# Second values and gates in the background of the attention items, queries split over 128 rows

## The chip, the cores and the metric

The kernel runs on one core of one Trainium2 chip. The metric is the device time of one launch in microseconds, the median of several runs, and less is better. The core's engines work side by side, each with its own queue of instructions: TensorE (PE; its weight loads are shown as PEld), VectorE (DVE), ScalarE (ACT), GpSimd (POOL) and SyncE (SP), which here issues most DMA transfers. Matmul results go to eight PSUM banks; everything else lies in SBUF.

## The reference, cut to what matters

A decoder of two layers over 512 tokens of width 1024. Layer 0 is a short gated convolution and a squared-ReLU MLP. Its output is normed and projected once to keys and values for three attention branches; layer 1 is the attention, followed by a second MLP and a last norm. The attention has 16 heads in 4 groups (4 heads share keys and values), head size 64.

```python
h   = rms_norm(x, kv_norm);  kv = h @ w_kv          # six parts of 256 columns: raw k, raw v, sel k, sel v, win k, win v
k_cmp, v_cmp = silu(blocks(raw + pe) @ phi_w1) @ phi_w2   # 31 blocks of 32 tokens, stride 16
q   = (rms_norm(x, g) @ w_qg[:, :1024]) * 64**-0.5
gates = sigmoid(rms_norm(x, g) @ w_qg[:, 1024:])    # three per head
o_b = softmax(q k_b^T + bias + mask) v_b            # b: compressed, selected, window
o   = gates[0]*o_c + gates[1]*o_s + gates[2]*o_w;   x += o @ w_o
```

With 512 tokens the top 16 of 8 blocks are all blocks, and the window is as long as the sequence, so the second and third branch are both full causal attention, with keys and values of their own.

## The kernel before

Each float32 operand is kept as a float16 high part and a float16 rest, and a product is made of three matmuls (hi x hi, hi x rest, rest x hi; `mm3`). Weights come in pieces of 128 x 1024 float32. `pieces` lists them in the order of use (L74 to L145); SP loads a piece to a staging buffer `wst` (three of them), ACT makes its high part `whi` (L232) and DVE its rest `wlo` (L233; four buffers each). `next_piece` hands out the next one, `ahead_fine` converts up to two pieces ahead, in steps of 512 columns up to the list's index `whole`. So the list and the order of the calls have to agree.

The attention (from L760) has a **lead-in** and an **item loop**. The lead-in (L1080) runs `keys(0)`, `keys(1)`, `queries(0)`, `values(0)`, `values(1)` and `gates()` to their ends. `keys` and `values` are of the two full branches: `values` makes 4 x 8 x 3 matmuls of 256 columns into two PSUM banks and evicts four 128 x 256 tiles to `VT` (ACT high part, DVE rest). `gates` makes 96 matmuls of 48 columns and evicts with Sigmoid on ACT into `GT`. During the lead-in, `abank` takes banks in turn from three pairs; afterwards always from the pair `a`.

The loop runs over 96 **items**. A `Full` item is one query block (128 tokens, index `qb`), one branch `br` and one, two or four heads; a `Cmp` item is one query block of the compressed branch for the eight heads of two groups. `items` (L1297) has the 22 Full items of group 0, those of group 1, then groups 2 and 3 with four Cmp items mixed into each. An item has five steps: `st0` scores (L1152, L1153), bias and minimum (DVE, L1160), Exp (ACT, L1162); `st1` transposes (L1168, PSUM bank `c`) and the high part on ACT (L1171); `st2` the rest on DVE (L1174); `st3` the product with the values (L1187 to L1189) and, at the last item of a query block, division and gates on DVE; `st4` the transposed output in `ot` once all branches of the block are in (`finish`). Iteration `i` emits st0 of item `i`, st1 of `i-2`, st2 of `i-3`, st3 of `i-4`, st4 of `i-6`.

Beside the items runs the **background** (L1303), a generator whose steps yield what they charge (0.65 for three matmuls of 512 columns; a step that names nothing is charged 0.1). Each iteration adds to `credit` and runs background until it is used up (L1334 to L1346); a "wait" sets the credit to zero. Its order: `raw(0)`, `queries(1)`, `phi(0)` in turn with `raw(1)`, `queries(2)`, `phi(1)`, `queries(3)`, and, when groups 0 and 1 are finished, `out_proj(0)`. `raw` projects raw keys or values and puts them, by transfers from `kr_hl`, into the tile `big` in the layout that `phi` (the compression MLP) reads as moving operand. `queries` projects a group's 256 query columns. `head` then makes each head's high part on ACT and the rest on DVE or POOL, 64 partitions at a time: the tile `Q` holds a head's high part in one half of the partitions and its rest in the other. Outside the lead-in the four `head` calls go to `later`, of which one runs per iteration. `queries(3)` waits with its eviction until the last Cmp item of groups 0 and 1 has been emitted, because `Q` has three buffers.

What is emitted in this order is then placed on the engines' queues by a scheduler that goes by that order as priority and by what is ready in its own plan.

Of the kernel before, what the change touches and what calls it, by code (L numbers as in the profile page):

```python
# [48 lines left out]
def body(ctx, tc, x, rel_bias, norm_mix, norm_mlp, mlp_w1, mlp_w2, a_w_in, a_conv_w, a_w_out,  # L49
# [75 lines left out]
    for part in (3, 5):  # L125
        block(w_kv, part * 256)
    cols(b_w_qg[0], 1024, 48, SW)
    block(w_kv, 0)
    block(b_w_qg[0], 256)

    for k in (0, 8):
        block(phi_k_w1, 0, SW, k, 4)
        cols(w_kv, 256, 256, SW, k // 2, 4)
        block(phi_k_w1, 0, SW, k + 4, 4)
    cols(phi_k_w2, 0, 64, SW, 0, 2)
    block(b_w_qg[0], 512)
# [623 lines left out]
    with pool("attn") as ap:  # L760
# [126 lines left out]
        def gates():  # L887
            w = next_piece()
            pg = abank()
            for t in range(4):  # L890
                for c in range(8):
                    lx = [u[:, c, t * 128:(t + 1) * 128] for u in xq]
                    o = pg[:, t * 48:(t + 1) * 48]
                    PE.matmul(o, lx[0], w[0][:, c], start=c == 0, stop=False)
                    PE.matmul(o, lx[0], w[1][:, c], start=False, stop=False)
                    PE.matmul(o, lx[1], w[0][:, c], start=False, stop=c == 7)
                yield
            for t in range(4):
                ACT.activation(GT[:, t], pg[:, t * 48:(t + 1) * 48], AF.Sigmoid, bias=zero, scale=rtok[:, 1, t:t + 1])
            DVE.tensor_scalar(GT, GT, SO / (SP * SV), None, op0=OP.mult)  # L900
            gc = GT[:, 0].rearrange("p (h b) -> p h b", b=3)[:, :, 0]
            DVE.tensor_scalar(gc, gc, any_, None, op0=OP.mult)
            yield


        def queries(g):
# [7 lines left out]
            def head(h):  # L914
# [3 lines left out]
                (POOL if g in (0, 3) else DVE).tensor_tensor(q[o, h], t[r, m], q[r, h], op=OP.subtract)  # L918
                done.add(f"q{g}.{h}")

            for m in range(2):
                DVE.tensor_tensor(t[:, m], po[m], rbq, op=OP.mult)
            for h in range(4):
                if lead_in[0]:
                    head(h)
                else:
                    later.append(lambda h=h: head(h))
# [5 lines left out]
        def raw(which):  # L933
# [3 lines left out]
            DVE.memset(kr[64:128, :, 0:4, S - 1:S], 0.0)  # L937
# [5 lines left out]
            for m in range(2):  # L943
# [6 lines left out]
                for s in range(2):  # L950
# [3 lines left out]
                    nc.sync.dma_start(kr[64:128, :, g, S - 32:S - 1], hl[r, :, 1:32])  # L954
# [72 lines left out]
        done = set()  # L1027
# [52 lines left out]
        for k in (keys(0), keys(1), queries(0), values(0), values(1), gates()):  # L1080
            drain(k)
# [50 lines left out]
        class Full:  # L1132
# [7 lines left out]
            def need(self):  # L1140
                return [f"q{self.g}.{self.heads[-1]}"]

# [64 lines left out]
        class Cmp:  # L1207
# [5 lines left out]
            def need(self):  # L1213
                return [f"q{2 * self.gp}.3", f"q{2 * self.gp + 1}.3", "cmp"]

# [82 lines left out]
        items += mixed(full(2), {4 + 3 * qb: Cmp(0, qb) for qb in range(4)})  # L1298
# [4 lines left out]
        def background():  # L1303
            yield from raw(0)
            yield from queries(1)
            yield from in_turn(phi(0), raw(1))
            yield from queries(2)
# [8 lines left out]

        lead = {1: 2, 2: 3, 3: 4, 4: 6}
        credit = 3.0
        for i in range(len(items) + 5):
            if i < len(items):  # L1320
                for k in items[i].need():
                    while k not in done:
                        if later:
                            later.pop(0)()
                        elif next(bg, "end") in ("wait", "end"):
                            raise RuntimeError(k)
# [7 lines left out]
            credit += 1.14 if i < 44 else 0.9 if i < 50 else 0.58  # L1334
# [3 lines left out]
            for part in ("stages", "background") if frees else ("background", "stages"):  # L1338
# [8 lines left out]
                for s in (1, 2, 3, 4):  # L1347
                    j = i - lead[s]
                    if 0 <= j < len(items) and (s, j) != (4, len(items) - 1):
                        getattr(items[j], f"st{s}")()  # L1350
# [177 lines left out]
```

## Time and profile before

| | |
|---|---|
| median of 3 runs | 1106.68 us (1106.1 to 1107.04) |
| profiled execution | 1106.44 us, of which span 1104.7 us |
| granted TensorE clock | 0.998 |
| lead-in of the attention | about 500 to 545 us of the span |
| item loop, first to last score matmul | 544.8 to 747.6 us |

The profile is that of one execution on the one core. Times within it count from the start of the span. [...] A row of a group gives line, engine, operation, output and inputs, shapes, count, then busy us, mean ns, and the idle time before with what ended it.

### The profile page before, as it was taken

How to read it: one execution, taken by the hardware profiler on the slowest of the kernel's cores; microseconds unless marked ns; L12 is line 12 of the kernel's file. 1: busy time of each engine (PE TensorE's matmuls, PEld its weight loads, DVE VectorE, ACT ScalarE, POOL GpSimd, SP SyncE). 2: the span in 40 equal slices, each digit the busy share in tenths (PEclk: the TensorE clock that was granted, in tenths of full speed). 3: DMA queues.
4: the chain of work that ended last, by engine and by line, in shares of the span. 5: the costliest groups of instructions: out<-in, count | busy, mean ns of one | idle time of the engine just before them, and what ended most of it. 6: DMA issues, size and time to landing. Idle time of an engine off the chain costs nothing. (4 is left out here: it accounts for less than half of the span.)

```text
span 1104.7 us, 20302 instructions
## 1 busy us (share of the span) xinstructions
PE 1087.0 (98%) x8112; PEld 704.9 (64%) x8112; DVE 897.3 (81%) x1594; ACT 584.0 (53%) x925; POOL 57.4 (5%) x74
## 2 busy tenths in 40 slices
PE   9999999999999999999999999999999999999997
PEld 4446644447884448875767676675444788445886
DVE  5897757987988767979488899996798798875786
ACT  5663245544333544447677887874655534352353
POOL 1000000000000000000100102211100000000022
PEclk9999999999999999999999999999999999999999
DMA  8353135633333333312352432011653333330222
GB/s 254 117 152 115 39 96 153 172 96 115 115 108 106 111 97 108 103 31 76 115 154 68 131 116 79 28 33 57 172 153 115 116 115 115 115 96 1 84 89 77
DMA packets 149710, 115.77 MB, mean 105 GB/s; under 512 B 8828, under 2 KB 146768, under 8 KB 149616
## 3 DMA queue, kind: packets, MB, share of 16 engines
q1 hardware_dynamic: 146720, 109.14, 33.0%
q10 hardware_dynamic: 2512, 4.70, 1.4%
q8 instruction: 64, 1.05, 0.4%
q0 software_dynamic: 384, 0.63, 0.2%
q14 instruction: 30, 0.25, 0.1%
HBM read 110.22 MB, written 2.14 MB: 102 GB/s over the span
## 5 line engine op out<-in xcount | busy, mean ns | idle before, releaser
L232 ACT ACTIVATE whi<-wst 128x1024 f16<-128x1024 f32 (+3 forms) x156 | 136.2, 887 | 120.8 <-PE b L387 37.4
L688 PEld LDWEIGHTS <-whi 128*128 128x128 f16 x1768 | 173.0, 98 | 20.4
L219 ACT ACTIVATE whi<-wst 128x1792 f16<-128x1792 f32 x70 | 118.2, 1696 | 124.6 <-DVE wst L160 55.5
L233 DVE SCALAR_TENSOR_TENSOR wlo<-wst,whi 128x1024 f16<-128x1024 f32 (+3 forms) x156 | 157.1, 1017 | 26.6 <-ACT whi L232 26.3
L388 PEld LDWEIGHTS <-wlo 128*128 128x128 f16 x976 | 95.5, 98 | 105.5 <-issue 0.7
L386 PEld LDWEIGHTS <-whi 128*128 128x128 f16 x976 | 95.7, 98 | 101.0 <-issue 0.9
L387 PEld LDWEIGHTS <-whi 128*128 128x128 f16 x976 | 95.5, 98 | 100.3 <-issue 0.3
L220 DVE SCALAR_TENSOR_TENSOR wlo<-wst,whi 128x1792 f16<-128x1792 f32 x70 | 141.0, 2018 | 15.4 <-ACT whi L219 15.4
L625 DVE TENSOR_TENSOR rl<-ml_z,rh 128x1792 f16<-128x1792 f32 x32 | 64.7, 2023 | 44.5 <-ACT rh L624 44.4
L688 PEld LDWEIGHTS <-wlo 128*128 128x128 f16 x884 | 86.5, 98 | 10.8 <-issue 0.4
L624 ACT ACTIVATE rh<-ml_z 128x1792 f16<-128x1792 f32 x32 | 54.3, 1696 | 60.2 <-DVE ml_z L166 60.2
L1162 ACT ACTIVATE at_p<-at_s,at_m 128x384 f32<-128x384 f32 (+3 forms) x128 | 70.9, 555 | 22.3 <-DVE at_m L1160 21.2
L388 PE MATMUL b<-xsh,wlo 128*128 128x512 f16 x208 | 78.8, 379 | 0.0
L387 PE MATMUL b<-xsl,whi 128*128 128x512 f16 x208 | 78.8, 379 | 0.0
L386 PE MATMUL b<-xsh,whi 128*128 128x512 f16 x208 | 78.8, 379 | 0.0
L386 PE MATMUL c<-xsh,whi 128*128 128x512 f16 x192 | 72.8, 379 | 0.0
L387 PE MATMUL c<-xsl,whi 128*128 128x512 f16 x192 | 72.8, 379 | 0.0
L388 PE MATMUL c<-xsh,wlo 128*128 128x512 f16 x192 | 72.8, 379 | 0.0
L158 DVE TENSOR_TENSOR wst<-wst 128x512 f32<-128x512 f32 x70 | 48.5, 695 | 26.5 <-DMA wst<-mlp_w_dram 25.2
L688 PE MATMUL a<-rh,whi 128*128 128x256 f16 x256 | 69.1, 273 | 0.0
L688 PE MATMUL a<-rh,wlo 128*128 128x256 f16 x256 | 69.1, 273 | 0.0
L688 PE MATMUL c<-rh,whi 128*128 128x256 f16 x252 | 68.7, 273 | 0.1
(388 smaller groups left out, 2686.8 us busy)
## 6 DMA issues: line engine op xcount, KB each, us to landing
wst<-mlp_w_dram SPq DMA_DIRECT2D x256, 256.0 KB, 3.4
wst<-a_w_in_dram SPq DMA_DIRECT2D x12, 512.0 KB, 3.8
wst<-w_kv_dram SPq DMA_DIRECT2D x12, 512.0 KB, 3.8
wst<-a_w_out_dram SPq DMA_DIRECT2D x8, 512.0 KB, 3.4
wst<-b_w_qg_dram SPq DMA_DIRECT2D x8, 512.0 KB, 3.7
wst<-b_w_o_dram SPq DMA_DIRECT2D x8, 512.0 KB, 3.4
T<-ext_d ACTq DMA_DIRECT2D x6, 528.0 KB, 3.9
wst<-a_w_in_dram SPq DMA_DIRECT2D x12, 256.0 KB, 3.0
```

The lines of the kernel that those rows point to most:

```text
L158: DVE.tensor_tensor(b[:, :, 4:7:2], b[:, :, 0:1].to_broadcast(two), b[:, :, 2:0:-1], op=OP.add)
L219: ACT.activation(hi, b[:, :, 1:], AF.Copy, scale=sc)
L220: lows[0] = DVE.scalar_tensor_tensor(lo, b[:, :, 1:], sc, hi, op0=OP.mult, op1=OP.subtract)
L232: ACT.activation(hi[:, s:e], w, AF.Copy, scale=sc)
L233: DVE.scalar_tensor_tensor(lo[:, s:e], w, sc, hi[:, s:e], op0=OP.mult, op1=OP.subtract)
L386: PE.matmul(ps, w[0], xs[0], start=start, stop=False, **k)
L387: PE.matmul(ps, w[0], xs[1], start=False, stop=False, **k)
L388: return PE.matmul(ps, w[1], xs[0], start=False, stop=stop, **k)
L624: ACT.activation(rh[0][:, p], z[:, 1:8], AF.Copy)
L625: DVE.tensor_tensor(rh[1][:, p], z[:, 1:8], rh[0][:, p], op=OP.subtract)
L688: mm = PE.matmul(acc7[i], wl if n == 1 else wh, xl if n == 2 else xh, stop=c == closes[i] and n == 2, start=c == 0 and n == 0 and not othe ...
L1162: self.weighed = ACT.activation(self.p[:, w], lg[:, w], AF.Exp, bias=mn[:, j:j + 1], scale=-1.0, accum_out=l[:, br * 4 + h:br * 4 + h + 1])
```

## The change

- The lead-in ends after `values(0)`. `values(1)` and `gates()` become the first parts of the background; a Full item's `st3` first asks for the values of its branch and, for branch 1, the gates (`need_last`, `have`). `gates` now yields a charge and converts weights ahead.
- The background's order is `values(1)`, `gates`, `queries(1)`, `raw(0)`, `phi(0)` in turn with `queries(2)`, `raw(1)`, `phi(1)`, `queries(3)`, `out_proj(0)`; the list of weight pieces follows.
- The credit per iteration is 1.25 up to item 53, 1.0 up to 63, then 0.75 (before: 1.14 up to 43, 0.9 up to 49, then 0.58).
- The four Cmp items of groups 0 and 1 stand behind Full items 9, 11, 14 and 16 of group 2 instead of 4, 7, 10 and 13.
- Queries of groups 1 to 3 are split over all 128 partitions, two heads at a time, into `kr_hl`, and four transfers put the halves into `Q`. Group 0's rests are still made per head, all on POOL.
- `raw` loses a memset and the third transfer of each group, which filled columns that no matmul reads.

```diff
     block(b_w_qg[0], 0)
-    for part in (3, 5):
-        block(w_kv, part * 256)
+    block(w_kv, 3 * 256)
+    block(w_kv, 5 * 256)
     cols(b_w_qg[0], 1024, 48, SW)
+    block(b_w_qg[0], 256)
     block(w_kv, 0)
-    block(b_w_qg[0], 256)
 
     for k in (0, 8):
         block(phi_k_w1, 0, SW, k, 4)
-        cols(w_kv, 256, 256, SW, k // 2, 4)
+        cols(b_w_qg[0], 512, 256, SW, k // 2, 4)
         block(phi_k_w1, 0, SW, k + 4, 4)
     cols(phi_k_w2, 0, 64, SW, 0, 2)
-    block(b_w_qg[0], 512)
+    block(w_kv, 256)
     block(phi_v_w1, 0, SW, 0, 16)
...
         def gates():
             w = next_piece()
+            cv = ahead_fine()
             pg = abank()
             for t in range(4):
                 for c in range(8):
+                    next(cv, None)
...
-                yield
+                yield 0.6
+            drain(cv)
...
                 ACT.activation(q[r, h], t[r, m], AF.Copy)
-                (POOL if g in (0, 3) else DVE).tensor_tensor(q[o, h], t[r, m], q[r, h], op=OP.subtract)
+                POOL.tensor_tensor(q[o, h], t[r, m], q[r, h], op=OP.subtract)
                 done.add(f"q{g}.{h}")
+
+            def two_heads(m, hl):
+                ACT.activation(hl[:, 2 * m], t[:, m], AF.Copy)
+                (POOL if g == 3 else DVE).tensor_tensor(hl[:, 2 * m + 1], t[:, m], hl[:, 2 * m], op=OP.subtract)
+
+            def put_heads(hl):
+                for s in range(2):
+                    r, o = slice(64 * s, 64 * s + 64), slice(64 - 64 * s, 128 - 64 * s)
+                    nc.sync.dma_start(q[r, s::2], hl[r, 0::2])
+                    nc.sync.dma_start(q[o, s::2], hl[r, 1::2])
+                done.update(f"q{g}.{h}" for h in range(4))
 
             for m in range(2):
                 DVE.tensor_tensor(t[:, m], po[m], rbq, op=OP.mult)
-            for h in range(4):
-                if lead_in[0]:
+            if lead_in[0]:
+                for h in range(4):
                     head(h)
-                else:
-                    later.append(lambda h=h: head(h))
+            else:
+                hl = ap.tile([128, 4, S], F16, name="kr_hl", bufs=1)
+                for m in range(2):
+                    later.append(lambda m=m: two_heads(m, hl))
+                later.append(lambda: put_heads(hl))
             yield
...
-            DVE.memset(kr[64:128, :, 0:4, S - 1:S], 0.0)
...
                     nc.sync.dma_start(kr[0:64, :, g, :], hl[r])
                     nc.sync.dma_start(kr[64:128, :, g, 0:S - 32], hl[r, :, 32:S])
-                    nc.sync.dma_start(kr[64:128, :, g, S - 32:S - 1], hl[r, :, 1:32])
...
-        for k in (keys(0), keys(1), queries(0), values(0), values(1), gates()):
+        for k in (keys(0), keys(1), queries(0), values(0)):
             drain(k)
...
+            def need_last(self):
+                return [f"v{self.br}"] + (["gates"] if self.br else [])
...
-        items += mixed(full(2), {4 + 3 * qb: Cmp(0, qb) for qb in range(4)})
+        items += mixed(full(2), {i: Cmp(0, qb) for qb, i in enumerate((9, 11, 14, 16))})
...
         def background():
+            yield from marked("v1", values(1))
+            yield from marked("gates", gates())
+            yield from queries(1)
             yield from raw(0)
-            yield from queries(1)
-            yield from in_turn(phi(0), raw(1))
-            yield from queries(2)
+            yield from in_turn(phi(0), queries(2))
+            yield from raw(1)
             yield from marked("cmp", phi(1))
...
+        def have(names):
+            for k in names:
+                while k not in done:
+                    if later:
+                        later.pop(0)()
+                    elif next(bg, "end") in ("wait", "end"):
+                        raise RuntimeError(k)
...
-            credit += 1.14 if i < 44 else 0.9 if i < 50 else 0.58
+            credit += 1.25 if i < 54 else 1.0 if i < 64 else 0.75
...
+                        if s == 3:
+                            have(items[j].need_last())
                         getattr(items[j], f"st{s}")()
```

More of the change, by code (lines that the diff above doesn't have):

```diff
@@ L1025, in phi @@
             drain(ahead())
-        done = set()
+        done = {"v0"}
         oT = {}
@@ L1214, in need, with need_last @@
                 return [f"q{2 * self.gp}.3", f"q{2 * self.gp + 1}.3", "cmp"]
+            def need_last(self):
+                return []
             def st0(self):
@@ L1320, in body @@
             if i < len(items):
[L1321 to L1326, printed above, removed]
+                have(items[i].need())
                 items[i].st0()
```

## The prediction

> **What bounds the kernel now.** The page comes first. TensorE (PE) is shown busy for 98% of the span, so a gain that isn't less matmul work has to come out of the rest.
>
> ```profile
> span 1104.7 us, 20302 instructions
> PE 1087.0 (98%) x8112; PEld 704.9 (64%) x8112; DVE 897.3 (81%) x1594; ACT 584.0 (53%) x925; POOL 57.4 (5%) x74
> ```
>
> The change touches the attention part alone, so the second view is the busy time by stretches of it. The columns are PE, weight loads, VectorE (DVE), ScalarE (ACT) and GpSimd (POOL), then the granted clock and the DMA share.
>
> ```profile
> 500.00:545.00 45.00, 45.00 (x393) 31.27 (x391) 31.55 (x62) 27.48 (x51) 5.22 (x4) 1.00 0.32 89
> 545.00:570.00 25.00, 24.27 (x194) 14.59 (x193) 18.36 (x59) 19.91 (x55) 0.00 (x0) 1.00 0.41 117
> 600.00:626.00 26.00, 24.45 (x262) 16.79 (x261) 22.02 (x74) 19.43 (x66) 0.73 (x1) 1.00 0.47 144
> ...
> 626.00:691.00 65.00, 62.64 (x793) 47.22 (x791) 63.99 (x178) 54.78 (x143) 10.36 (x14) 1.00 0.34 100
> ...
> 691.00:706.00 15.00, 12.65 (x144) 9.09 (x142) 13.39 (x41) 13.84 (x38) 6.63 (x6) 1.00 0.01 2
> ...
> 545.00:747.00 202.00, 194.47 (x2198) 139.04 (x2197) 183.91 (x542) 160.93 (x438) 26.27 (x36) 1.00 0.30 88
> ```
>
> The lead-in (500 to 545) holds PE full while DVE has 13 us free. The item loop (545 to 747) is the reverse: PE is shown idle for 202 - 194.5 = 7.5 us, and from 626 to 691 DVE works 63.99 of 65 us: there DVE, not PE, ends the work. The largest hole per us is 691 to 706, 2.35 us of 15. What PE stands still for:
>
> ```profile
> PE c L1168 <- DVE at_pl L1174: 3.5, 7, 1.1
> ...
> PEld c L1168 <- issue: 5.0, 8, 1.5
> PEld c L1168 <- DVE at_pl L1174: 2.3, 6, 0.6
> ```
>
> Mostly it is a transpose (L1168) that needs a PSUM bank which DVE (L1174) still reads. The 7.5 us are a lower bound: a matmul's shown length runs past the start of the next.
>
> ```profile
> 498.33 0.38 PE L386 MATMUL a<-xsh,whi 128*128 128x512 f16 x1
> 498.55 0.38 PE L387 MATMUL a<-xsl,whi 128*128 128x512 f16 x1
> ```
>
> A 512-column matmul is shown for 0.38 us, and the next starts after 0.22, so each stop hides up to 0.16 us. With about 40 stops (the three rows alone have 21) that is 6.4 us more. Everything that filling can win is 7.5 to 14 us, estimated from these rows.
>
> **The change, part by part.**
>
> *Second values and gates leave the lead-in.* Their PE work:
>
> ```profile
> 542.28 0.27 PE L876 MATMUL b<-whi,xsl 128*128 128x256 f16 x1
> 542.39 0.19 PE L894 MATMUL c<-whi,xqh 128*128 128x48 f16 x1
> ...
> L874 PE MATMUL b<-whi,xsh 128*128 128x256 f16 x32 | 8.7, 272 | 0.0
> ...
> L1152 PE MATMUL b<-KD,Q x128: 217/298/380, 544.8 to 747.6; 128*128 128x384 f16 x32, 128*128 128x128 f16 x32, 128*128 128x512 f16 x32, 128*128 128x256 f16 x32
> ...
> L884 DVE SCALAR_TENSOR_TENSOR VT<-b,rtok,VT x4: 477/481/482, 537.9 to 544.8; 128x256 f16<-128x256 f32 x4
> ```
>
> The values are 3 x 32 matmuls at 0.11 us from start to start, 10.5 us; the gates run from 542.39 to the first item at 544.8, 2.4 us. So the items start 12.9 us earlier, and the same 12.9 us of PE work is spread among them. This alone moves no end; it gains as much as it fills stops. What DVE takes over with it is small: 4 evictions of 0.48 us, 1.9 us, and two short gate operations.
>
> *The rate.* From L1334 and the charges that each background step yields, I count the background per iteration. Before, iterations 44 to 63 grant 6 x 0.9 + 14 x 0.58 = 13.5 us of it; after, 10 x 1.25 + 10 x 1.0 = 22.5. Counted back from iteration 65 (692.5, quoted below) at some 2.1 us each, they lie from about 648 to 691, in the stretch in which DVE ends the work. With 9 us more PE work beside the same items, its 42 us of DVE work and the 5.5 us of phi(1)'s conversions that move in (8 x 0.69) lie in some 52 us: 91% instead of 98%. Up to iteration 43 the rate rises by 0.11 only, and PE is nearly full there already. I take that of the stops from 600 to 691 (1.55 + 2.36 us shown, some 7 with what the records hide) about 2 remain: **-5.0 us**.
>
> *Queries split over 128 rows.*
>
> ```profile
> L917 ACT ACTIVATE Q<-q_t x16: 613/627/631, 523.9 to 696.8; 64x512 f16<-64x512 f32 x16
> L918 POOL TENSOR_TENSOR Q<-q_t,Q x8: 1152/1156/1496, 524.7 to 697.6; 64x512 f16<-64x512 f32 x8
> L918 DVE TENSOR_TENSOR Q<-q_t,Q x8: 684/686/687, 581.9 to 647.4; 64x512 f16<-64x512 f32 x8
> ...
> L407 ACT ACTIVATE kr_hl<-q_t x4: 612/618/623, 559.8 to 623.1; 128x512 f16<-128x512 f32 x4
> ```
>
> Half the partitions cost as much as all of them (0.627 against 0.618 us). For groups 1 and 2 DVE loses 4 x 0.686 = 2.7 us, little more than the moved evictions bring, so DVE's total stays; ACT loses 6 x 0.62 = 3.7 us. Group 3 needs two POOL operations (1.16 us) instead of four. Added are 4 transfers per group on SP's queue, between the weight loads; they are costed with the next part. Behind a transfer that waits for POOL or DVE stand those loads, which run two pieces ahead. For all of this I take 0, from -1 (DVE) to +2 (group 3, whose queries now pass two POOL operations and four transfers, some 2.3 + 2.6 + 2.3 us, within the five iterations before their first use).
>
> *The hole.* Background of group 3 waits for the last block of groups 0 and 1.
>
> ```profile
> 692.52 3.61 POOL L918 TENSOR_TENSOR Q<-q_t,Q 64x512 f16<-64x512 f32 x3 [3.48 <-issue]
> ```
>
> This is iteration 65, in the hole at 691. Before, no background is issued in iterations 64 to 68; after, the compressed items lie later (the last at 64 instead of 61) and none is issued in 65 to 71. Five iterations cost 2.35 us shown, about 3.5 with the hidden part; seven cost 4.9 by the same rate: **+1.4**, from 0 to +3.
>
> *The gates among the items.* Sigmoid and Exp need different tables on ACT.
>
> ```profile
> 544.01 0.46 ACT L883 ACTIVATE VT<-b,rtok 128x256 f16<-128x256 f32 x1
> 544.49 1.28 ACT L899 ACT_TABLE_LOAD   x1
> 545.78 1.24 ACT L899 ACTIVATE GT<-c,zero,rtok 128x48 f32<-128x48 f32 x4
> 547.04 1.28 ACT L1162 ACT_TABLE_LOAD   x1
> ```
>
> Before there are two loads; after, Exp, Sigmoid, Exp: three. The burst of 1.28 + 1.24 + 1.28 = 3.8 us now stands in front of Exps that transposes wait for. ACT works 19.9 of 25 us at that place, and a transpose comes two iterations (4.6 us) after its Exp is queued, so most is covered: +0.6, from 0 to the whole 3.8. [...]
>
> *Raw keys and values, and what stands behind them.* One memset and 8 small transfers go, of 24.
>
> ```profile
> 558.16 1.98 DVE L946 TENSOR_TENSOR q_t<-a,rb 128x512 f32<-128x512 f32 x2
> ...
> L952 SPq DMA_DIRECT2D big<-kr_hl x8: 590/606/659, 561.9 to 627.3; - x8
> L954 SPq DMA_DIRECT2D big<-kr_hl x8: 601/610/1197, 563.3 to 628.6; - x8
> ...
> DMA to landing us min/median/max: 1.8/2.3/5.1
> ...
> L386 PE MATMUL e<-big,whi x64: 232/233/234, 580.5 to 653.4; 128*128 128x155 f16 x64
> ```
>
> Each transfer holds SP for 0.61 us. Before, phi(0) starts at 580.5, 22 us after the eviction of raw(0) begins, with queries(1) between; phi(1) has queries(2) between. After, phi(0) shares its iterations with queries(2), and phi(1) follows raw(1) directly. From eviction to landing I count 3.7 us to the first transfer, 8 x 0.65 and 2.3: 11.2 us. What may lie in that time is the items' work, and the order is not the written one:
>
> ```profile
> 500.90 0.07 DVE L979 MEMSET phi_h<- 128x16 f16 x1
> ```
>
> This memset belongs to phi(0), written behind the whole lead-in, and runs 80 us early. So work that is ready is placed ahead of what waits. I take +0.8; the ends are 0 and 10.8 (worked out under the second rival).
>
> *Two more handovers of bank pair a* (values to gates, gates to queries): each may hold PE until DVE has evicted 2 x 0.48 us; they are covered in part by the items, +0.3 from 0 to 2.
>
> Sum: -5.0 + 0 + 1.4 + 0.6 + 0.8 + 0.3 = **-1.9 us**, and with DVE's share of the query split (up to -1, since it falls where DVE ends the work) -2.9. I take -2.9. The profiled execution took 1106.44 us (span 1104.7 and 1.7 around it), 0.24 below the median 1106.68. Forecast: 1106.44 - 2.9 = **1103.5 us**.
>
> **The rivals.** *Same time:* the stops only move. DVE and ACT have no less to do in sum; the first 40 iterations were nearly free of stops (0.73 us in 545 to 570) and get burst, handovers and waits, while the hole grows. With the hole at +3, the burst at +1.5 and the handovers at +1 instead of the values above, the sum is +0.3: about 1106.5 us. For it: the hole is the worst place already and the change lengthens it. Against it: DVE at 98% between 626 and 691 clearly gets relief.
>
> *Slower:* phi's operands arrive too late. During 11.2 us after raw(1) nothing of the background but phi(1) is near, and queries(3) cannot pass it because the weight buffers (four) are held by phi's pieces. The rows for what DVE and PE do in it:
>
> ```profile
> 561.13 1.29 DVE L409 TENSOR_TENSOR kr_hl<-q_t,kr_hl 128x512 f16<-128x512 f32 x2
> ...
> L233 DVE SCALAR_TENSOR_TENSOR wlo<-wst,whi 128x512 f16<-128x512 f32 x26 | 17.3, 687 | 2.7 <-ACT whi L232 2.7
> L1174 DVE SCALAR_TENSOR_TENSOR at_pl<-c,at_ph 128x384 f16<-128x384 f32 x32 | 17.7, 552 | 4.8 <-ACT at_ph L1171 4.8
> L1160 DVE CUSTOM_DVE_ANT_0 at_s<-b,T 128x384 f32<-128x384 f32 x32 | 17.4, 544 | 0.9 <-PE b L1153 0.8
> ...
> 614.32 1.03 DVE L946 TENSOR_TENSOR q_t<-a,rb 128x512 f32<-128x512 f32 x1
> ...
> 653.71 0.52 PE L1168 MATMUL c<-ident,at_p 128*128 128x128 f32 x3
> 654.41 0.33 PE L1152 MATMUL b<-KD,Q 128*128 128x384 f16 x1
> ```
>
> DVE spends 1.98 + 1.29 = 3.3 on the eviction and 4 x 0.69 = 2.8 on two pieces; the 5.1 left carry some 4.6 items at 0.55 + 0.55. PE's part of such an item is 1.03 us (653.71 to 654.41, and two matmuls of 0.16), 4.7 in all, so PE stands 6.5 us. At phi(0) half of queries(2) (8 x 0.65 = 5.2 us) fills in as well and 1.3 remain: 7.8. That is a lower price: at raw(1) of before, with DVE full, the steps took from 614.3 to 628.6 + 0.6 + 2.3, and 15 us without the four transfers that go, instead of 11.2. Between, at 13 us, I get 3 more, 10.8. Some 3 return because DVE is ahead afterwards: -2.9 - 0.8 + 10.8 - 3 = +4.1, 1110.5 us. The sign turns at 3.7 us of such standstill that doesn't return. For it: the order of the parts; against it: 8 transfers less, and an order that fills by readiness. [...]
>
> **How the numbers follow.** Forecast 0.45, same 0.27, slower 0.28. A measurement of this kernel can tell about 0.2%, 2.2 us, from no change. The forecast's own range is 1100 to 1105: all stops in the stretch gone and no hole added on one side, the upper ends of burst and hole on the other. The range that reaches to the other cases is 1099 to 1111: below, 7.5 us of filled stops; above, the slower rival. Faster by over 0.2% gets 0.45, within it 0.27, slower 0.28.
>
> **What would show it.** The first item's matmul (L1152) starts near 532 instead of 544.8. In the stretch of the second compressed half PE's idle falls to about 1 us while DVE is shown at about 91%. One more table load on ACT, with Sigmoid between Exps. A stretch without background before the first output projection, 7 iterations and over 3 us of idle. The slower rival shows as a stop of PE of several us just ahead of the first matmuls from big, ended by the transfers from kr_hl. If PE's idle in the loop stays near 7.5 us, the forecast's main term is wrong; if the lead-in shows stops, my reading of the 12.9 us is.

## The result and the profile after

| | before | after |
|---|---|---|
| median | 1106.62 us (6 runs, 1106.1 to 1107.04) | 1115.16 us (6 runs, 1114.77 to 1115.38) |
| profiled execution, span | 1106.44, 1104.7 us | 1114.77, 1113.0 us |
| ratio of the runs | | 1.0077, 95% interval 1.0064 to 1.0090 |

The change makes the kernel 8.5 us slower. The forecast was 3 us faster; the time lies above its range, and above the 1111 us of the range that takes in the rivals. The page of after, first lines and one group of PE:

```profile
span 1113.0 us, 20326 instructions
...
PE 1090.2 (98%) x8112; PEld 706.6 (63%) x8112; DVE 898.1 (81%) x1588; ACT 585.9 (53%) x922; POOL 56.4 (5%) x72
...
L386 PE MATMUL b<-xsh,whi 128*128 128x512 f16 x208 | 78.8, 379 | 2.3 <-DVE X L591 2.3
```

There are as many matmuls as before, and DVE works 0.8 us more; nearly all of the difference is time that PE loses (worked out below). In after's code the lines have moved: L1152 of before is L1170, L1168 is L1186, L1160 is L1178, L1162 is L1180, L1171 is L1189, L1174 is L1192, L1187 to L1189 are L1205 to L1207, L899 is L902, L946 is L962, L952 and L953 are L968 and L969. The busy time by stretches (PE, weight loads, DVE, ACT, POOL, granted clock, DMA):

```profile
487.00:532.00 45.00, 45.00 (x273) 26.51 (x271) 36.85 (x71) 30.11 (x54) 5.21 (x4) 1.00 0.30 87
532.00:557.00 25.00, 24.09 (x319) 19.89 (x317) 16.65 (x54) 19.95 (x47) 0.00 (x0) 1.00 0.28 86
...
650.00:661.00 11.00, 8.10 (x100) 6.18 (x98) 9.96 (x30) 7.58 (x21) 1.10 (x1) 0.84 0.46 104
661.00:685.00 24.00, 23.14 (x288) 17.41 (x286) 20.04 (x54) 17.92 (x48) 2.15 (x5) 1.00 0.42 132
685.00:696.00 11.00, 11.00 (x141) 8.04 (x137) 10.56 (x26) 8.05 (x19) 2.81 (x4) 1.00 0.43 141
696.00:711.00 15.00, 12.98 (x136) 9.31 (x134) 14.76 (x49) 12.34 (x36) 5.73 (x5) 1.00 0.15 36
```

The lead-in (487 to 532) is full. One stretch stands out, 650 to 661: PE idle for 2.9 of 11 us, and the granted clock at 0.84. The part without background (696 to 711) is idle for 2.0 of 15 us, about the 2.35 of before.

The idle column hides up to 0.16 us per stop, as the prediction said. For all comparisons below I therefore worked out PE's **lost time** from the starts of its matmuls: what the time to the next start exceeds the usual step of that shape (0.215 us for 512 columns, 0.109 for 256 and so on), summed over the items that ran meanwhile (their score matmuls mark the borders). A matmul that runs at half the granted clock counts as lost time too. In us, with the span of the profiled execution; "end" is the first 40 us behind the loop:

```
                              items of the loop
                 span    0-18  18-42  42-60  60-72  72-96   end   sum
before          1104.7    1.1    3.2    3.2    5.5    2.4   0.2  15.6
after           1113.0    3.3    3.8    7.7    4.0    2.3   2.7  23.8
e1_rot          1110.8    3.3    3.8    7.6    4.1    2.3   0.3  21.4
e2_order        1111.2    3.3    3.8    4.1    4.9    2.3   2.6  20.9
e3_tanh         1114.4    1.7    4.3    8.0    4.0    2.3   4.3  24.8
e4_three        1107.1    1.7    4.3    3.8    4.9    2.3   0.2  17.3
e1b_rot_fill    1108.4    3.3    3.8    2.7    7.1    2.4   0.2  19.4
e5_bank_e       1109.7    1.2    4.3    7.6    4.0    2.3   0.2  19.7
e6_fill         1109.8    1.2    4.3    2.7    7.1    2.7   0.2  18.2
b2_raw          1105.1    1.1    3.0    3.2    5.5    2.4   0.2  15.4
b1_split_raw    1102.3    1.1    1.6    2.5    4.7    2.4   0.2  12.5
c1_rate         1108.8    1.0    4.1    6.0    5.5    2.2   0.2  19.0
c2_old_order    1110.5    3.3    3.7    3.1    8.3    2.2   0.3  21.0
c3_values       1104.0    0.9    3.8    2.9    4.9    2.2   0.2  14.9
d1_places       1105.1    1.1    1.6    2.7    5.4    3.9   0.2  14.8
d2_credit       1110.5    1.0    5.8    6.3    5.2    2.0   0.6  20.9
d3_val_places   1105.9    0.9    3.8    3.1    5.5    2.3   0.2  15.8
d4_val_early    1107.3    0.6    2.8    8.0    3.2    2.9   0.2  17.7
f1_gates_lead   1108.7    0.6    3.6    6.7    6.5    2.3   0.2  19.9
f2_gates_order  1106.8    0.6    3.5    3.9    6.5    2.5   0.2  17.2
```

Span less sum is 1089 to 1092 us in every row: the lost time accounts for the differences within about 2 us, and for the 8.3 us of span between before and after fully (8.2). Against before the change loses 2.2 more in items 0 to 18, 0.6 in 18 to 42, 4.5 in 42 to 60 and 2.5 at the end, and wins 1.5 in 60 to 72. In these executions the granted clock falls to half for 3.4 us in after, e1_rot, e5_bank_e, c2_old_order and d2_credit, for 6.8 in d4_val_early and for 10.2 in e3_tanh, in the others not before the kernel's last 8 us; each 3.4 us at half clock hold up to 1.7 us of lost time (see the last section). The three large losses have causes that the trace shows.

**Items 48 to 60: phi(1) behind raw(1).** The timeline of after, SP's issues first, then PE's stops and the first matmul of phi(1) (the bracket gives the idle time and what ended it):

```profile
653.50 0.60 SPq L968 DMA_DIRECT2D big<-kr_hl  x1
...
658.09 0.61 SPq L969 DMA_DIRECT2D big<-kr_hl  x1
...
651.81 0.32 PE L1170 MATMUL b<-KD,Q 128*128 128x384 f16 x1 [1.02 <-DVE at_m L1178]
655.09 0.32 PE L1170 MATMUL b<-KD,Q 128*128 128x384 f16 x1 [1.73 <-DVE at_m L1178]
...
663.17 0.23 PE L386 MATMUL e<-big,whi 128*128 128x155 f16 x1
...
648.70 1.98 DVE L962 TENSOR_TENSOR q_t<-a,rb 128x512 f32<-128x512 f32 x2
```

From the eviction at 648.70 to the first product from big at 663.17 PE has only items, each of which waits for its own chain through DVE and ACT. No row names the transfers; what is seen is scores waiting for a bank b, until DVE has taken the minimum (`at_m`) of an earlier item out of it, because nothing else is there to do. DVE is busy for 9.96 of 11 us, the 91% that the forecast wanted; from 650 to 696 it is 40.6 of 46 us, 88%.

**Items 6 to 18: the tables change four times.** The groups of table loads from 525 to 760 (count, busy us, mean ns, idle before), after:

```profile
L1180 ACT ACT_TABLE_LOAD x3 | 3.8, 1283 | 0.1
L902 ACT ACT_TABLE_LOAD x2 | 2.6, 1283 | 0.0
```

Five, where before had two; the first is Exp's own. ACT's timeline of the other four, and PE's two stops beside them:

```profile
551.18 1.28 ACT L902 ACT_TABLE_LOAD   x1
552.48 0.39 ACT L902 ACTIVATE GT<-a,zero,rtok 128x48 f32<-128x48 f32 x1
552.77 0.48 ACT L1189 ACTIVATE at_ph<-c 128x384 f16<-128x384 f32 x1
553.26 1.28 ACT L1180 ACT_TABLE_LOAD   x1
...
556.22 1.28 ACT L902 ACT_TABLE_LOAD   x1
557.52 0.95 ACT L902 ACTIVATE GT<-a,zero,rtok 128x48 f32<-128x48 f32 x3
558.36 0.49 ACT L1189 ACTIVATE at_ph<-c 128x384 f16<-128x384 f32 x1
558.87 1.28 ACT L1180 ACT_TABLE_LOAD   x1
...
553.98 0.52 PE L1186 MATMUL c<-ident,at_p 128*128 128x128 f32 x3 [0.91 <-DVE at_pl L1192]
558.52 0.38 PE L386 MATMUL a<-xqh,whi 128*128 128x512 f16 x1 [0.74 <-ACT GT L902]
```

The four Sigmoids do not run in one burst. One is ready first, Exps slip in behind it, and the tables change four times, 4 x 1.283 = 5.1 us of ACT. PE stops at 553.98, and at 558.52 because the next background part wants the bank pair that ACT still reads for GT.

**The end: two pairs in one bank.** The timeline of after behind the last output projection:

```profile
784.01 0.38 PE L386 MATMUL c<-xsh,whi 128*128 128x512 f16 x1
784.23 0.38 PE L387 MATMUL c<-xsl,whi 128*128 128x512 f16 x1
786.86 0.38 PE L386 MATMUL b<-xsh,whi 128*128 128x512 f16 x1 [2.26 <-DVE X L591]
...
781.77 0.68 DVE L591 SCALAR_TENSOR_TENSOR X<-a,X 128x512 f32<-128x512 f32 x1
...
786.13 1.28 DVE L591 SCALAR_TENSOR_TENSOR X<-b,X 128x512 f32<-128x512 f32 x2
```

Outside the loop banks are taken from `"aabbcc"[turn[0] % 6]`. Before, the lead-in took 11 of them; now, with three fewer, the last pair of the output projection falls on b, which the MLP wants too, and PE stands until DVE has evicted it.

### The profile page after: what moved, and what is told of

Read it like the earlier page. It is cut to its first block, busy times and chain, and to the rows that moved or that the text cites. A ratio compares the mean times of both kernels' runs of the same rounds, so it can differ in the third digit from the quotient of the medians.

```text
span 1113.0 us, 20326 instructions
## 1 busy us (share of the span) xinstructions
PE 1090.2 (98%) x8112; PEld 706.6 (63%) x8112; DVE 898.1 (81%) x1588; ACT 585.9 (53%) x922; POOL 56.4 (5%) x72
## 5 line engine op out<-in xcount | busy, mean ns | idle before, releaser
L688 PEld LDWEIGHTS <-wlo 128*128 128x128 f16 x884 | 86.5, 98 | 10.8 <-issue 0.4
L1180 ACT ACTIVATE at_p<-at_s,at_m 128x384 f32<-128x384 f32 (+3 forms) x128 | 70.9, 555 | 27.0 <-DVE at_m L1178 26.5
L688 PE MATMUL c<-rl,whi 128*128 128x256 f16 x252 | 68.7, 273 | 0.0
```

What stands on the lines that cost most here:

```text
L688: mm = PE.matmul(acc7[i], wl if n == 1 else wh, xl if n == 2 else xh, stop=c == closes[i] and n == 2, start=c == 0 and n == 0 and not othe ...
L1180: self.weighed = ACT.activation(self.p[:, w], lg[:, w], AF.Exp, bias=mn[:, j:j + 1], scale=-1.0, accum_out=l[:, br * 4 + h:br * 4 + h + 1])
```

## The experiments

Theory A at the outset: the loss is these three places, and moving the work is otherwise neutral. Theory B: the stops move, so a mended place gives its gain back later.

**Rotation alone** (`e1_rot`). To the change:

```diff
         lead_in[0] = False
+        turn[0] += 3
```

> The changed kernel with the turn of PSUM banks moved on by three at the end of the lead-in, nothing else. With values(1) and gates out of the lead-in, three banks less are taken there, and the last pair of the second output projection falls on banks b and b, which the first pair of the MLP behind it also wants. Theory (the 2.4 us stop at 786.9 us is this collision): the stop goes, 1112.7 us, and the loop up to 755 us stays as it is. Rival (the stop comes from VectorE being late with the last residuals, whatever the bank): the stop stays at 1.5 us or more, 1114.5 to 1115.2 us.

1112.54 us, ratio 1.0053 (1.0038 to 1.0068), 2.6 under the change. The stretch 780 to 790, after and then this run:

```profile
780.00:790.00 10.00, 7.74 (x37) 3.43 (x36) 10.00 (x15) 7.27 (x11) 2.00 (x3) 1.00 0.37 88
```

```profile
780.00:790.00 10.00, 10.00 (x48) 4.52 (x47) 10.00 (x16) 7.47 (x12) 1.99 (x3) 1.00 0.36 89
```

PE is full, and the loop's lost time is unchanged. This part is shown.

**Order alone** (`e2_order`). To the change:

```diff
-            yield from in_turn(phi(0), queries(2))
-            yield from raw(1)
+            yield from in_turn(phi(0), raw(1))
+            yield from queries(2)
             yield from marked("cmp", phi(1))
```

(and the list of weights to match).

> The changed kernel with the old order of these parts: phi(0) in turn with raw(1), then queries(2), then phi(1), and the list of weights to match; all else as changed. Theory (phi(1) directly behind raw(1) leaves TensorE with the items alone for 13 us, from 650 to 663): the stop in front of phi(1) goes, about 5 to 6 us, 1109.5 us. Rival (the denser background as such makes VectorE late, wherever the parts stand): stops of the same size appear elsewhere between 600 and 690, 1113 us or more.

1112.53 us, ratio 1.0055 (1.0038 to 1.0072): 2.6 won, where about 5.5 was expected. The wait for phi(1) is gone, but queries(2) now comes just in time for item 44, the first of group 2, and a new wait stands there:

```profile
PE b L1170 <- DMA Q<-kr_hl: 1.5, 1, 1.5
...
DMA to landing us min/median/max: 2.4/3.4/3.7
```

The first row is from the waits of this run's stretch 648 to 657, the second from the transfers into Q there. The transfers of the split queries, which before did not exist, are what PE waits for.

**Tanh for Sigmoid** (`e3_tanh`). The gate as (tanh(x/2) + 1)/2, with the halved scale in `rtok`; to the change:

```diff
-                ACT.activation(GT[:, t], pg[:, t * 48:(t + 1) * 48], AF.Sigmoid, bias=zero, scale=rtok[:, 1, t:t + 1])
-            DVE.tensor_scalar(GT, GT, SO / (SP * SV), None, op0=OP.mult)
+                ACT.activation(GT[:, t], pg[:, t * 48:(t + 1) * 48], AF.Tanh, bias=zero, scale=rtok[:, 1, t:t + 1])
+            DVE.tensor_scalar(GT, GT, 1.0, 0.5 * SO / (SP * SV), op0=OP.add, op1=OP.mult)
```

> The changed kernel with the gates computed as 0.5 + 0.5 tanh(x/2) on the same 4 tiles, since Tanh runs among the Exps without a table load in phi. Theory (four table loads of 1.28 us at the gates stop TensorE for some 2.2 us between 550 and 565): no load there, 1113.0 us. Rival (the stops there are the handover of bank pair a, and the loads are covered): 1114.5 us or more.

1115.41 us, ratio 1.0079 (1.0064 to 1.0094). The table loads from 525 to 760 in this run:

```profile
L1180 ACT ACT_TABLE_LOAD x1 | 1.3, 1283 | 0.0
```

Four loads go, and nothing is won, although items 0 to 18 lose 1.6 us less. The handover of bank pair a remains, items 18 to 60 lose 0.8 more, and the end 1.6 more. The end is no stop that moved. From 780 to 790, beside the row of after above:

```profile
780.00:790.00 10.00, 7.75 (x29) 3.14 (x28) 10.00 (x15) 6.91 (x11) 2.23 (x4) 0.83 0.36 102
```

PE is busy as long as in after (7.74), but starts 29 matmuls instead of 37, at a mean clock of 0.83. So this run is no evidence for theory B. Two of its four runs have a mean granted clock of 0.997, as the profiled execution of after, and took 1114.2 and 1114.7 us, 0.5 to 0.9 less than the change; the two with 0.994 and 0.996 took 1116.2 and 1116.5.

**All three** (`e4_three`: the edits of e1_rot, e2_order and e3_tanh).

> The three edits of the runs before it together: banks moved on by three, the old order of phi and raw, the gates by Tanh. Theory (these three are the loss, and the even background gains behind them): 1115.2 - 2.4 - 5.5 - 2.2 = 1105.1 us, below the kernel before by about 1.5 us. Rival (the background at the new rate loses by itself): 1108 us or more.

1108.97 us, ratio 1.0019 (1.0010 to 1.0028), 6.2 under the change where the single edits sum to 5.0. Still slower than before: the three places are not the whole.

**Filling the wait, and a bank of their own for the gates.** `e1b_rot_fill` is the change with the turned banks and the first 8 steps of queries(3) between raw(1) and phi(1) (the list of weights to match):

```diff
+            q3 = queries(3)
+            for _ in range(8):
+                yield next(q3)
             yield from marked("cmp", phi(1))
-            yield from queries(3)
+            yield from q3
```

> The kernel with the banks moved on by three, and the first half of queries(3) (8 steps, 5.2 us of matmuls) taken between raw(1) and phi(1); the rest of queries(3) stays behind phi(1). Against 1112.5 us for the banks alone. Theory (TensorE waits before phi(1) for the transfers of raw(1), with only the items to do): the 5.2 us of matmuls fill most of the 7.6 us that items 48 to 60 lose, 1108.5 us. Rival (in that stretch VectorE is the limit, so more matmuls there only move the stops): 1111.5 us or more.

1110.96 us, ratio 1.0049 (1.0034 to 1.0064). Items 42 to 60 lose 2.7 instead of 7.6, items 60 to 72 lose 7.1 instead of 4.1: queries(3) is missing there. A stop that moved, 3.0 of 4.9 us; up to 1.7 of the 4.9 is the clock, which fell to half there in e1_rot and did not in this run. Then `e5_bank_e`, turned banks and Tanh with the gates' products in a bank of their own, and `e6_fill`, the same with the filled wait:

```diff
-            pg = abank()
+            pg = bank("e")
```

> Banks moved on by three, gates by Tanh, and the gates' products in bank e, which nothing uses at that time, instead of pair a. Against 1112.5 us for the banks alone. Theory (what the gates cost among the items is table loads and the handover of pair a, 1.5 us each, of which Tanh alone took the first and left the second at 1.49 us): both stops go, items 6 to 18 lose under 0.7 us instead of 3.2, 1109.5 us. Rival (what is saved early is lost again in front of phi(1), where the items are ahead of the background anyway): 1111.5 to 1112.5 us.

> All of it: banks moved on by three, gates by Tanh in bank e, half of queries(3) before phi(1). Theory (the losses of the change are these four stops, and the denser background wins some 3 us elsewhere): 1105.5 us, below the kernel before by 1.2. Rival (the losses move to the stretch without background before the first output projection and to the items' own pace): 1107.5 us or more.

1111.74 (1.0048, 1.0035 to 1.0062) and 1110.54 us (1.0037, 1.0023 to 1.0051). The gates' place is mended, items 0 to 18 lose 1.2, and the second, expected at 1105.5, shows the same 7.1 in items 60 to 72.

**The parts that do not move work.** `b1_split_raw` is before with the query split (`two_heads`, `put_heads`) and raw's cut, as in the change's diff:

> The kernel before with two parts of the change alone: queries of groups 1 to 3 split over 128 rows and put in place by transfers, and raw without its memset and third transfers. Lead-in, order, rate and places as before. Theory (these parts are worth 0 to 1 us, as VectorE loses 2.7 us of work where it is the limit): 1105.7 to 1106.7 us. Rival (the transfers come too late for the first scores of a group): 1108 us or more.

1104.01 us, ratio 0.9978 (0.9969 to 0.9987), 2.7 faster than before and the fastest of all kernels here. Raw's cut alone, `b2_raw`:

```diff
-            DVE.memset(kr[64:128, :, 0:4, S - 1:S], 0.0)
...
-                    nc.sync.dma_start(kr[64:128, :, g, S - 32:S - 1], hl[r, :, 1:32])
```

> Before with one part of the change alone: raw's memset and its eight third transfers go; queries stay per head. Together with the query split this gave 1104.0 (2.7 under before). If the gain is the transfers' (raw's columns land earlier, phi(0) starts earlier): 1104 to 1104.5. If it is the split's (DVE has fewer rests to make): 1106 to 1106.7.

1106.5 us, 0.9998 (0.9988 to 1.0007): nothing. The gain is the split's. The page of b1_split_raw:

```profile
PE 1087.0 (99%) x8112; PEld 705.6 (64%) x8112; DVE 893.6 (81%) x1588; ACT 579.8 (53%) x919; POOL 54.8 (5%) x72
```

DVE has 3.7 us less to do than before and ACT 4.2, and the lost time falls from 11.9 to 8.8 in items 18 to 72. So the rest of the change costs 11 us.

**Credits, places, order, values, gates.** `c1_rate`: to b1_split_raw, credits and places of the Cmp items as in the change, with no work moved:

```diff
-            credit += 1.14 if i < 44 else 0.9 if i < 50 else 0.58
+            credit += 1.25 if i < 54 else 1.0 if i < 64 else 0.75
-        items += mixed(full(2), {4 + 3 * qb: Cmp(0, qb) for qb in range(4)})
+        items += mixed(full(2), {i: Cmp(0, qb) for qb, i in enumerate((9, 11, 14, 16))})
```

> Before with query split, raw's cut, and the change's credits and places of the Cmp items; lead-in and order of the background as before, so no work moves into the loop. It tells the rate from the moved work. Theory A (an even rate relieves the stretch in which DVE ends the work, as the prediction's first term had it): about 1101.5, 2.5 under the 1104.0 of split and cut alone, and the stops from 600 to 691 shrink. Theory B (the stops of that stretch only move, above all into the part without background before the first output projection): 1104 to 1106.

1110.6 us (1.0045, 1.0030 to 1.0059), 6.6 over b1_split_raw. The main term of the prediction was worth minus 5; without moved work it is worth plus 6.6. Then `c2_old_order`, the change with turned banks and the old order behind values(1) and gates (and the list of weights to match):

```diff
             yield from marked("v1", values(1))
             yield from marked("gates", gates())
+            yield from raw(0)
             yield from queries(1)
-            yield from raw(0)
-            yield from in_turn(phi(0), queries(2))
-            yield from raw(1)
+            yield from in_turn(phi(0), raw(1))
+            yield from queries(2)
```

> The change, with three added to the turn of banks, and with the order of before behind the gates: values(1), gates, raw(0), queries(1), phi(0) in turn with raw(1), queries(2), phi(1). Beside c1_rate only values(1) and the gates move. Theory A (order and gates are what costs, moving itself is free): the phi(1) wait of about 5.5 us goes from the 1112.5 of the turned banks, 1107. Theory B (13 us of matmuls more in the loop cost by handovers of bank pair a and by items that come later against the same DVE and ACT work): 1109 or more.

1112.13 us (1.0050, 1.0035 to 1.0065): by theory A 1107. With the gates among the items the order is worth 0.4 (1112.54 of e1_rot against this run); without them it will turn out to be worth 4.5 (f1_gates_lead). And `c3_values`, the same with the gates in the lead-in (the list of weights to match, two added to the turn):

```diff
-        for k in (keys(0), keys(1), queries(0), values(0)):
+        for k in (keys(0), keys(1), queries(0), values(0), gates()):
...
-            yield from marked("gates", gates())
```

> As c2_old_order, but the gates stay in the lead-in (two added to the turn of banks): values(1) alone moves. The gates cost what c2_old_order has above this one. Theory A (table loads and handover of the gates cost 2.2 us): 2 us under c2_old_order, 1105. Theory B (this shows up later anyway, as with Tanh): the same as c2_old_order within 0.7 us.

1106.64 us (1.0000, 0.9991 to 1.0010). The gates among the items cost 5.5 us here, of which 2.4 stand in items 0 to 18 and 3.4 in 60 to 72, where the clock drops once (below). Against c1_rate, values(1) in the loop *wins* 4.0 us, which fits if it is the work that the larger credits ask for. Against b1_split_raw it is still 2.6 behind.

Credits and places one by one on b1_split_raw: `d1_places` has the second pair of lines of c1_rate's diff, `d2_credit` the first:

> Split and cut (1104.0) with the change's places of the four Cmp items of groups 0 and 1 alone; credits as before. c1_rate, which has places and credits, took 1110.6. Theory A (the later Cmp items cost: the part without background before the first output projection is longer and they crowd the end of group 2): 1108 or more. Theory B (the credits cost: work handed out early is missing later): 1104 to 1105.

> Split and cut with the change's credits alone; places as before. Theory A: 1104 to 1105.5; theory B: 1108 or more. If both single edits lie near 1107, they add.

1106.94 us (0.9999, 0.9990 to 1.0009) and 1111.56 (1.0041, 1.0027 to 1.0055): 2.9 and 7.6 over b1_split_raw, and 6.6 together. They do not add. The credits are the larger part. Of the 8.4 us that d2_credit loses more than b1_split_raw, 3.8 stand in items 42 to 60, where the work that was handed out early is missing, but 4.2 stand earlier, in items 18 to 42. The longest stop there, from its waits between 600 and 612:

```profile
PE c L1180 <- DVE at_pl L1186: 1.7, 1, 1.7
```

Transposes (L1180 in this kernel) wait for a bank that DVE still has to read, while DVE works on weight rests (one takes 1.23 us at 605.72); the clock falls to half behind it (last section). With values(1) moved, the later places help by 1.0: `d3_val_places` is c3_values with the places of before.

> c3_values (values(1) moved, order of before, the change's credits; 1106.6) with the places of before. Theory A: about 1103; theory B: 1106.6 again.

1107.66 us (1.0009, 1.0000 to 1.0019). And `d4_val_early`, values(1) moved at the pace of before:

```diff
-            credit += 1.25 if i < 54 else 1.0 if i < 64 else 0.75
+            credit += 1.38 if i < 44 else 0.9 if i < 50 else 0.58
```

> As d3_val_places, with credits of 1.38 up to item 43 and then as before (0.9, 0.58), so that the 10.5 us of values(1) are spread over the first 44 items alone and the rest of the loop keeps the pace of before. If moving work into the loop is itself free, as the prediction had it, this stands at the 1104.0 of split and cut; if it costs by handovers and by work that finds no stop, 1105.5 or more.

1109.23 us (1.0025, 1.0016 to 1.0034), 5.2 over b1_split_raw. Nearly all of it is one place, item 44 again; waits, the transfers into Q from issue to landing around it, and the two us from 654 behind it:

```profile
PE b L1171 <- DMA Q<-kr_hl: 4.4, 1, 4.4
...
DMA to landing us min/median/max: 4.3/6.5/6.8
...
654.00:656.00 2.00, 2.00 (x14) 1.74 (x13) 0.69 (x3) 1.66 (x3) 0.00 (x0) 0.50 0.00 2
```

The wait is 4.4 us; behind it PE runs at half clock, which adds to the 8.0 us lost in items 42 to 60. So moving work is not free: a part that comes later meets the item that needs it.

Last, the gates' price in the change's own order: `f1_gates_lead` is the change with c3_values' edit of gates and turn, `f2_gates_order` that with the order of e2_order.

> The change with the gates back in the lead-in and two added to the turn of banks: values(1) alone moves, in the change's own order, credits and places. Against the 1112.5 of the turned banks alone it prices the gates among the items, under another order than c3_values did (there 5.5 us). If the price is the gates' own stops (2.2 us in items 6 to 18): 1110.3. If it is that and the later stops that they shift: 1107 to 1108.

> As f1_gates_lead, with phi(0) in turn with raw(1), queries(2), and then phi(1) (the order of e2_order), so that no part stands directly behind the transfers it waits for. Rotation, gates and phi(1) are mended; what is left over split and cut (1104.0) is the price of values(1) in the loop and of credits and places. By sums of the single edits (1112.5 - 2.6 - 2.2 to 5.5): 1104.4 to 1107.7; a version that beats split and cut would stand under 1103.5.

1111.11 us (1.0040, 1.0025 to 1.0055) and 1108.84 (1.0020, 1.0010 to 1.0029). In this order the gates cost 1.4, not 5.5: items 0 to 18 win 2.7, items 60 to 72 lose 2.4. With rotation, gates and phi(1) all mended, 4.8 us over b1_split_raw remain. Beside c3_values, which has the order of before, the change's order adds 4.5 (f1_gates_lead); raw(0) behind queries(1) instead of ahead of it is the only difference between f2_gates_order and c3_values, and adds 2.2.

What this settles: theory A's three places are real. The rotation's price stands by itself: the end loses 2.6 us or more in the three kernels with a shortened lead-in and unturned banks (after, e2_order, e3_tanh), and at most 0.6 in all others. One chain of runs, each one part of the change further, leads from b1_split_raw to the change: credits and places plus 6.6 (c1_rate), values(1) minus 4.0 (c3_values), order plus 4.5 (f1_gates_lead), gates plus 1.4 (e1_rot), rotation plus 2.6, in all 11.1. On another way through the same parts the prices differ (gates 1.4 or 5.5, order 0.4 or 4.5, places plus 2.9 or minus 1.0). Theory B's reason, that the stop turns up at the next place that has no background at hand, is seen in e1b_rot_fill; for the other combinations it is argued, and drops of the clock have a part in the differences. What stays open is a rule by which each stop of a combination could be named ahead; the 2.6 us between c3_values and b1_split_raw were not taken apart further.

## Why the prediction was wrong, step by step

- **Lead-in and start of the items** ("earlier by 12.9"): right. The scores' first and last start, after:

```profile
L1170 PE MATMUL b<-KD,Q x128: 219/318/508, 531.5 to 755.1; 128*128 128x384 f16 x32, 128*128 128x128 f16 x32, 128*128 128x512 f16 x32, 128*128 128x256 f16 x32
```

  13.3 us earlier, and the loop that was 202.8 us long (544.8 to 747.6) is 223.6: of the 20.8 more, 12.9 are the moved work, 6.0 lost time (the columns 0 to 96, less the part behind the last score), and 2 are not assigned.
- **Fill of stops, -5.0**: the step that failed. The loss from 600 to 691 does not fall to 2 of 7. Items 36 to 66 (626 to 691 of before) lose 10.0 us instead of 5.2, 7.6 of them in items 48 to 60. I counted granted work per iteration and DVE's share. The share came out (91% from 650 to 661, 88% to 696), but PE stood all the same: granted credit is no work if the next part waits for something, and the items alone run at the speed of their own chain DVE, ACT, PE. c1_rate and d2_credit show the sign: the larger credits without moved work cost 6.6 and 7.6 us instead of winning 5.
- **phi behind raw, +0.8**: the slower rival's mechanism. From 650 to 661 5.6 us are lost, up to 1.7 of them by the clock; the rival's lower price for phi(1) was 6.5, its price with phi(0) 10.8, which was too high. With other work there (e1b_rot_fill) items 42 to 60 lose 2.7 instead of 7.6. "An order that fills by readiness" was the wrong reason against it: what is ready must exist, and with queries(2) already used up nothing did. Removing the wait alone (e2_order) returns 2.6 only: queries(2) then meets its own deadline (1.5 us).
- **Slower rival, 1110.5**: right sign and place, 4.7 us short. It kept the -5.0 of the fill and did not have the rotation's 2.6; its 10.8 of standstill, too high, hid part of both.
- **Gates, +0.6 with three loads**: mis-sized. Five loads, since the Sigmoids were torn apart, and 2.2 us lost in items 0 to 18, the handover of pair a at 558.52 included, for which I had +0.3. By runs 1.4 to 5.5.
- **Hole, +1.4**: it did not grow. Items 66 to 72 lose 3.8 us, before 3.9.
- **Query split, 0 to -1**: mis-sized. Alone it wins 2.5 (b1_split_raw against b2_raw). What it takes off the engines was about right (2.7 of DVE and 3.7 of ACT forecast; 3.7 and 4.2 less than before on the page, raw's memset included); its worth was not, since I set it against the moved evictions. What I did not price is the other side: its transfers are a new last step before a group's first item, 1.5 and 4.4 us of PE where queries come just in time.
- **Raw's cut**: nothing, as b2_raw shows; it was not given a price of its own.
- **Not seen at all: the bank rotation, 2.6 us.** Taking work out of the lead-in changes a counter that code some 250 us later reads.

## What to carry to other kernels

Ask of each background part two questions: what does it wait for, and which item waits for it; a count of work per iteration answers neither, and a share of a busy engine below 100% does not mean that PE is fed. A stop that is filled by taking work from elsewhere is only gained if the other place did not need that work: measure mends together, since their single prices do not add, and compare the granted clocks before a difference of 1 or 2 us is put down to an edit. When a part of a sequence is removed, look for every round-robin counter that runs on behind it.

## What the hardware showed

**The clock dropped after short stops, not after all.** With the stops of 650 to 656, PE's granted clock falls to half for 3.4 us. In windows of two us, after:

```profile
654.00:656.00 2.00, 0.83 (x5) 0.47 (x5) 2.00 (x7) 0.71 (x3) 0.01 (x1) 1.00 0.53 121
656.00:658.00 2.00, 2.00 (x19) 1.37 (x17) 2.00 (x6) 1.08 (x3) 0.00 (x0) 0.51 0.82 188
658.00:660.00 2.00, 2.00 (x32) 1.99 (x31) 1.02 (x3) 1.28 (x4) 0.00 (x0) 0.64 0.87 198
```

The clock column is the third from the right. At half clock products of 64 columns start 0.053 us apart (658.04 to 658.36), at 1.00 0.029 (659.54 to 659.74), so 3.4 us do about the work of 1.7, and up to 1.7 of the 5.6 us lost there are the clock's. The drop doesn't follow from the stop alone. The same stop, first in d2_credit, then in c1_rate:

```profile
606.00:608.00 2.00, 0.21 (x2) 0.10 (x1) 2.00 (x5) 1.03 (x3) 0.00 (x0) 1.00 0.78 237
608.00:610.00 2.00, 1.83 (x18) 1.18 (x19) 1.84 (x6) 1.31 (x5) 0.11 (x1) 0.76 0.82 242
610.00:612.00 2.00, 2.00 (x11) 1.18 (x10) 0.27 (x1) 0.00 (x0) 0.61 (x1) 0.50 0.15 50
```

```profile
606.00:608.00 2.00, 0.20 (x1) 0.10 (x1) 2.00 (x5) 1.04 (x4) 0.00 (x0) 1.00 0.86 241
608.00:610.00 2.00, 1.96 (x24) 1.50 (x25) 1.84 (x5) 1.18 (x5) 0.24 (x1) 1.00 0.76 227
610.00:612.00 2.00, 2.00 (x16) 1.32 (x15) 0.71 (x3) 0.38 (x1) 0.48 (x1) 1.00 0.17 60
```

PE stands 1.8 of 2 us in both; in one the clock drops behind it, in the other it stays at 1.00. One kernel does both: of c1_rate's five runs three have a mean granted clock of 0.998 or 0.999 and took 1110.0 to 1110.6 us, two have 0.997 and took 1112.3 and 1113.2. The time at half clock is 3.4 us in after, d2_credit and c2_old_order; stops of under 2 us (1.73 in after, 1.7 in d2_credit) came before it, and c1_rate has such a stop with no drop behind it. What else decides it was not shown. In c2_old_order such a drop falls into items 60 to 72:

```profile
686.00:688.00 2.00, 0.72 (x5) 0.54 (x6) 2.00 (x3) 1.30 (x3) 1.14 (x1) 1.00 0.00 0
...
690.00:692.00 2.00, 2.00 (x12) 0.74 (x11) 1.39 (x3) 0.36 (x2) 0.95 (x1) 0.50 0.80 234
```

Its 3.4 us at half speed (689 to 692.4) are up to 1.7 of the 5.5 us that the gates cost there, which is one reason why prices do not add.

**A change of tables cost ACT its load and no more.** At each of the four loads above (after, 551.18, 553.26, 556.22 and 558.87) the load takes 1.28 us; it starts within 0.02 us of the end of the instruction before it, and the ACTIVATE behind it starts 0.02 us after the load.
